# Hybrid decoder layer on one core: the order of the gating values, the layer norm by halves, chunk and attention steps by two token tiles, and staging of the last operands

## The chip, the cores and the metric

The kernel runs on one core of one Trainium2 chip. The metric is device time in microseconds of one launch; lower is better. The kernel before was timed three times: 2019.73, 2021.77 and 2022.76 us, so its median is 2021.77 us. One further execution was profiled.

## The reference, cut to what matters

One layer over 2048 tokens of 1024 features, all fp32. Two mixers share one input projection, one output projection and a residual; a SwiGLU block and a final norm follow.

```python
n = rms_norm(h, norm1_w)
q, k, v, g_lr, g_out, su, sv = split(n @ w_in)      # 256,256,512,16,512,512,512 columns
log_a = log_sigmoid(g_lr @ w_gate_up + b) / 16
# gated linear attention, 4 heads, chunks of 64 tokens
b = cumsum(log_a, in chunk); q_dec = q*exp(b); k_inv = k*exp(-b); k_end = k*exp(b_last-b)
o = causal(q_dec k_inv^T) v + q_dec S_prev          # S = exp(b_last)*S + k_end^T v, chunk by chunk
o_gla = rms_norm_per_head(o) * silu(g_out)
# spatial gating, 4 groups of 128 channels, chunks of 128 tokens
o_sg = gelu(su) * (tril(w_s) @ layer_norm_per_group(gelu(sv)) + b_s)
h = h + concat(o_gla, o_sg) @ w_out
h = h + (silu(n2 @ w_gate) * (n2 @ w_up)) @ w_down  # n2 = rms_norm(h); d_ff = 2816
return rms_norm(h, final_norm_w)
```

## The kernel before, in words

**Products.** Every fp32 operand is split into a high part (a cast on ACT, L103) and a low part (a subtraction on DVE, L104); a product is three matmuls, lines L124, L125 and L126 in turn. A matmul of 512 columns follows the one before after 0.227 us. The low part of a weight tile (`wlo`) is wanted by L125 or L124 of its first product, so TensorE waits for both ACT and DVE of each tile. Weight tiles come by DMA into `raw` (three slots), are split into a pool of four pairs, and are prepared in the order in which a list, `block_tiles`, names them.

**Stages.** The tokens are four blocks of 512, each four token tiles of 128. Blocks 0 and 1 go through `mix` and the output projection, then through gate, up and down together; blocks 2 and 3 likewise. Gate, up, down and (in blocks 1 to 3) the value and output-gate columns use a seven-product scheme (Winograd's form of Strassen's) on halves of the operands; the product numbers are `m`, taken for the values and the gate in the order 1, 2, 7, 6, 4, 5, 3. One product there is 24 matmuls with two weight tiles of 12.

**`mix`, in the order in which TensorE takes it in blocks 1 to 3.** First half of the gating values `sv` with the low-rank gate; the decay; the K pair of column tiles; the Q pair; the second half of `sv` (`second_half`, 96 matmuls of 256 columns); the seven products of values `v` and output gate `gw`; the `su` column pairs (`gate_pair`), between whose tiles the attention steps stand; the output projection. In block 0 values, second half and gate are plain products.

**Side work on DVE.** Behind the Q pair DVE scales the scans (L501 to L508), applies exponentials to Q and K (L516, L517) and writes `left` (L539). `sv_norm` (L611, L612, then the inverse root, which is L130 on DVE and L131 on POOL, then L616) normalises `sv`, one token tile a step. Products m=2, 4 and 5 are drained by DVE adds (L647, L653, L657); m=5 and m=3 accumulate in the same PSUM buffers, so m=3 waits for L657.

**Chunk and attention steps.** One `chunks` step per token tile: 16 hardware matmuls k_end^T v (L568), eight state updates on DVE (L577), 16 score matmuls (L584), two predicated copies into `left` (L588). The steps are a generator started by the drain of m=4 and advanced as tiles are used (`tick`); what is left is run by `finish` ahead of `su`. `attend` likewise: 16 matmuls (L690), ACT squares, the root on POOL, four scalings (L698), and two steps later four transposes (L677) into `mixT`, which the output projection reads (`mixTl` is its low part). L717 multiplies the normalised `sv` with the spatial weights.

**Order and last product.** The generators and a Tile scheduler fix the order on each engine; each engine then takes its instructions strictly in that order, and SP issues the DMAs. In the last `down` the a operand and the b operand (`load`, L916 and L921) both come through the three `raw` slots; hi and lo parts lie in a pool of 16 large tiles (`bigt`). The last product but one fetches up to five units ahead, since its operands and those of the last stay loaded.

Of the kernel before, what the change touches and what calls it, by code (L numbers as in the profile page):

```python
# [8 lines left out]
F32 = mybir.dt.float32  # L9
# [6 lines left out]
P = 128  # L16
D = 1024
T = 2048
NB = 512
# [14 lines left out]
def hybrid_block(ctx, tc, x, norm1_w, w_in, w_gate_up, b_gate_up, gla_norm_w, sg_ln_w, sg_ln_b,  # L34
# [15 lines left out]
    def ps():  # L50
        return psp.tile([P, 512], F32, name="ps", tag="ps")
# [384 lines left out]
    def block_tiles(blk, first):  # L436

        def vg(m, kk):
            at = {1: (0, C_V), 2: (4, C_V), 3: (4, C_GOUT)}.get(m)
            if at:  # L440
                return tok_load(w_in, [(at[1], 512)], at[0] + 2 * kk, 2)
            return load_w([vd[{5: 0, 7: 1, 4: 2, 6: 3}[m], 2 * kk:2 * kk + 2].rearrange("k p c -> p k c")], 2, 512)

        tiles = [] if first else tok_tiles(w_in, first_cols, 3)
        tiles += col_tiles(w_in, 256) + col_tiles(w_in, 0)
        second = tok_tiles(w_in, [(C_SV + 256, 256)], 4)
        if blk == 0:
            tiles += tok_tiles(w_in, [(C_V, 512)]) + second + tok_tiles(w_in, [(C_GOUT, 512)])
        else:
            tiles += second + [lambda m=m, kk=kk: vg(m, kk) for m in VG_ORDER for kk in range(2)]  # L450
        for i in range(2):
            tiles += col_tiles(w_in, C_SU + i * 2 * P)
        return tiles + tok_tiles(w_out, [(0, 512)], order=OUT_ORDER) + tok_tiles(w_out, [(512, 512)])

    def mix(blk, nT, first_w):
# [71 lines left out]
        def mine(hh):  # L527
            return slice(hh * DK, (hh + 1) * DK)
# [30 lines left out]


        def chunks():
            for t in range(TT):
                pu = [ps(), ps()]
                for c in range(2):
                    rows = slice(c * CH, (c + 1) * CH)
                    for h in range(HEADS):
                        p, hh = h // 2, h % 2
                        nc.tensor.matmul(pu[c][hh * DK:(hh + 1) * DK, p * DV:(p + 1) * DV],  # L568
                                         lhsT=kend[rows, t, p, hh * DK:(hh + 1) * DK],
                                         rhs=v[rows, t, h * DV:(h + 1) * DV], start=True, stop=True)  # L570
                for c in range(2):
                    n = 2 * t + c
                    for p in range(2):
                        for hh in range(2):
                            rows = mine(hh)
                            new = right(n + 1)[rows, hh, p] if n + 1 < NB // CH else state[rows, p]
                            nc.vector.scalar_tensor_tensor(new, right(n)[rows, hh, p], dec[rows, p, n:n + 1],  # L577
                                                           pu[c][rows, p * DV:(p + 1) * DV], ALU.mult, ALU.add)
                pq = [ps(), ps()]
                for p in range(2):  # L580
                    for c in range(2):
                        ts = slice((2 * t + c) * CH, (2 * t + c + 1) * CH)
                        for hh in range(2):
                            nc.tensor.matmul(pq[hh][other(hh), (2 * p + c) * CH:(2 * p + c + 1) * CH],  # L584
                                             lhsT=kinv[mine(hh), p, ts], rhs=left[mine(hh), hh, p, ts], start=True, stop=True)
                for hh in range(2):
                    rows = other(hh)
                    nc.vector.copy_predicated(left[rows, hh, :, t * P:(t + 1) * P].rearrange("q p (c i) -> q p c i", i=CH),  # L588
                                              keep_i[rows].unsqueeze(1).unsqueeze(1).to_broadcast([CH, 2, 2, CH]),
                                              pq[hh][rows, :4 * CH].rearrange("q (p c i) -> q p c i", c=2, i=CH))  # L590
                yield

        def chunks_start():
            values_put()
# [7 lines left out]
            tok_group(w_in, [(C_SV + 256, 256)], nT, ks=4,  # L602
                      done=lambda t, acc: nc.scalar.activation(sv[:, t, 256:512], acc[:, :256], AF.Gelu))

        def sv_norm():
            for t in range(TT):
                st = sm.tile([P, 4, 6], F32, name="bst")
                mv = sm.tile([P, 4, 2], F32, name="mv")
                rs = sm.tile([P, 4], F32, name="rs")
                for g in range(4):  # L610
                    nc.vector.bn_stats(st[:, g, :], sv[:, t, g * P:(g + 1) * P])  # L611
                    nc.vector.bn_aggr(mv[:, g, :], st[:, g, :])  # L612
                rsq(rs, mv[:, :, 1], 1, 4)
                for g in range(4):
                    sl = sv[:, t, g * P:(g + 1) * P]
                    nc.vector.tensor_scalar(sl, sl, mv[:, g, 0:1], rs[:, g:g + 1], ALU.subtract, ALU.mult)  # L616
                yield


        def gate_scale(t):  # L620
# [7 lines left out]
        if halves is None:  # L628
            tok_group(w_in, [(C_V, 512)], nT, done=lambda t, acc: nc.scalar.copy(v[:, t, :], acc))
            g_chunks = chunks_start()  # L630
            second_half()
            g_svn = start(sv_norm())
            gw = bigt(F32, "gw")
            tok_group(w_in, [(C_GOUT, 512)], nT, done=gate_done)
        else:
            second_half()
            g_svn = start(sv_norm())
            finish(g_half)
            gw = bigt(F32, "gw")
            started = []  # L640
# [21 lines left out]

            pair_product(halves, VG_ORDER, {1: 0, 6: 0, 5: 0, 3: 0, 2: 1, 7: 2, 4: 2}, drain)
            g_chunks = started[0]
        finish(g_chunks)
        finish(g_svn)


        mixT = Act(KD, "mixT")

        def attend():
            oms = []
            for t in range(TT + 2):
                if t >= 2:
                    pt = ps()
                    for h in range(HEADS):
                        nc.tensor.transpose(pt[:, h * P:(h + 1) * P], oms[t - 2][:, h * DV:(h + 1) * DV], ident)  # L677
                    mixT.put(0, t - 2, pt)
                if t >= TT:
                    yield  # L680
                    continue
                ss = sm.tile([P, HEADS], F32, name="ss")
                om, sq = tpt("om"), tpt("sq")
                oms.append(om)
                pos = [ps(), ps()]
                for p in range(2):
                    for hh in range(2):
                        for c in range(2):
                            n = 2 * t + c
                            nc.tensor.matmul(pos[hh][c * CH:(c + 1) * CH, p * DV:(p + 1) * DV],  # L690
                                             lhsT=left[:, hh, p, n * CH:(n + 1) * CH], rhs=right(n)[:, hh, p], start=True, stop=True)
                for h in range(HEADS):
                    p, hh = h // 2, h % 2
                    nc.scalar.activation(sq[:, :DV], pos[hh][:, p * DV:(p + 1) * DV], AF.Square, accum_out=ss[:, h:h + 1])
                rsq(ss, ss, DV, HEADS)
                for h in range(HEADS):
                    p, hh = h // 2, h % 2
                    nc.vector.scalar_tensor_tensor(om[:, h * DV:(h + 1) * DV], pos[hh][:, p * DV:(p + 1) * DV], ss[:, h:h + 1],  # L698
                                                   gw[:, t, h * DV:(h + 1) * DV], ALU.mult, ALU.mult)
                yield  # L700

        g_att = start(attend())

# [19 lines left out]
                split(h, l, mx)  # L723

        for i in range(2):
            gate_pair(i, col_pair(nT))
        return mixT, g_att, hx

    def residual(hx, dh, acc, t):
# [170 lines left out]
    def down(s):  # L900
# [9 lines left out]
            a = bigt(F32R, name).rearrange("p (x a) b -> p x a b", x=2)  # L910
            return a[:, 0, :k], a[:, 1, :k]

        def load(spare=False):
            m, j, k = grans.pop(0)
            raw = view(rawp, F32, "raw", k, NB)
            nc.sync.dma_start(raw, ad[s][m - 1, j:j + k].rearrange("j p t -> p j t"))  # L916
            a = unit_parts("aop", k)
            split(*a, raw)
            if spare:
# [22 lines left out]
        def run(nxt):  # L942
# [52 lines left out]
            for m in order:  # L995
# [156 lines left out]
```

## Time and profile before

| | |
|---|---|
| median of three runs | 2021.77 us |
| profiled execution, own time | 2024.96 us |
| its span | 2023.0 us |
| TensorE (PE) busy | 1977.1 us, 98% |
| VectorE (DVE) busy | 1503.8 us, 74% |
| ScalarE (ACT) busy | 890.4 us, 44% |
| GpSimd (POOL) busy | 92.2 us, 5% |
| mean granted TensorE clock | 0.995 |
| DMA engines, mean busy share | 50% |

The profiled execution is 3.2 us above the median and 2.0 us longer than its span. A row of a timeline gives the start, the busy time, the engine, the line, and in brackets the idle time just before it with what ended it. PEclk is the share of full clock granted in a stretch.

### The profile page before, as it was taken

What the parts mean: (1) busy time and instruction counts of PE and PEld (TensorE: products, weight loads), DVE (VectorE), ACT (ScalarE), POOL (GpSimd) and SP (SyncE); (2) the same over time, 40 slices, a digit from 0 to 9 for tenths busy, and PEclk for the clock granted to TensorE, in tenths of its full rate; (3) what the DMA queues carried; (4) which work ended last, traced back from release to release, by engine and by line L of the source; (5) the groups of instructions that cost most, each with busy time, mean ns of one, the idle gap of its engine ahead of it and who ended that gap; (6) DMA issues with size and microseconds to landing.
All of it is one profiled execution on the core that took longest, in us unless ns stands there. A gap on an engine that the chain in (4) does not pass through costs nothing. (4 is left out here: it accounts for less than half of the span.)

```text
span 2023.0 us, 26612 instructions
## 1 busy us (share of the span) xinstructions
PE 1977.1 (98%) x9837; PEld 1646.7 (81%) x9837; DVE 1503.8 (74%) x2529; ACT 890.4 (44%) x1454; POOL 92.2 (5%) x102
## 2 busy tenths in 40 slices
PE   7999999999999999999999999999999999999997
PEld 6878977888888888888788788788888888888886
DVE  5676988798887777655798768859977876866466
ACT  4534745453333333433565536446433333334334
POOL 1011100000000000000110102000000000000000
PEclk9999999999999999999999999999999999999999
DMA  7553585526653324865655534723332332367555
GB/s 233 167 202 101 198 249 195 182 89 203 209 162 99 125 89 142 292 196 185 238 177 160 174 116 160 215 85 119 122 107 86 126 101 85 124 209 253 195 165 178
DMA packets 216719, 329.28 MB, mean 163 GB/s; under 512 B 16599, under 2 KB 117645, under 8 KB 215566
## 3 DMA queue, kind: packets, MB, share of 16 engines
q1 hardware_dynamic: 216590, 327.59, 50.0%
q8 instruction: 77, 1.26, 0.3%
q14 instruction: 52, 0.43, 0.1%
HBM read 246.27 MB, written 77.07 MB: 160 GB/s over the span
## 5 line engine op out<-in xcount | busy, mean ns | idle before, releaser
L103 ACT CAST whi<-raw 128x1024 fp32r<-128x1024 f32 (+2 forms) x209 | 211.3, 1011 | 357.0 <-PE ps L125 143.1
L104 DVE TENSOR_TENSOR wlo<-raw,whi 128x1024 fp32r<-128x1024 f32 (+2 forms) x209 | 243.7, 1171 | 130.7 <-ACT whi L103 124.9
L124 PE MATMUL ps<-whi,aop 128*128 128x512 f32 x552 | 215.1, 390 | 1.2 <-DVE aop L104 1.2
L125 PE MATMUL ps<-wlo,aop 128*128 128x512 f32 x552 | 214.8, 389 | 0.6 <-DVE wlo L104 0.6
L126 PE MATMUL ps<-whi,aop 128*128 128x512 f32 x552 | 214.8, 389 | 0.0
L103 ACT CAST op<-sw 128x512 fp32r<-128x512 f32 x176 | 107.4, 622 | 200.0 <-DVE sw L787 180.0
L104 DVE TENSOR_TENSOR aop<-raw,aop 128x1024 fp32r<-128x1024 f32 x84 | 95.2, 1134 | 99.5 <-ACT aop L103 99.0
L104 DVE TENSOR_TENSOR op<-sw,op 128x512 fp32r<-128x512 f32 x176 | 120.0, 685 | 38.0 <-ACT op L103 37.6
L103 ACT CAST aop<-raw 128x1024 fp32r<-128x1024 f32 x84 | 82.0, 979 | 138.1 <-DMA raw<-ad 137.0
L124 PE MATMUL ps<-whi,nTl 128*128 128x512 f32 (+2 forms) x392 | 129.0, 329 | 3.4 <-DVE nTl L104 3.4
L125 PE MATMUL ps<-wlo,nTh 128*128 128x512 f32 (+2 forms) x392 | 127.4, 325 | 0.0
L126 PE MATMUL ps<-whi,nTh 128*128 128x512 f32 (+2 forms) x392 | 127.4, 325 | 0.0
L124 PEld LDWEIGHTS ps<-whi,aop 128*128 128x128 f32 x552 | 103.6, 188 | 23.1 <-ACT junk L136 1.6
L125 PEld LDWEIGHTS ps<-wlo,aop 128*128 128x128 f32 x552 | 103.6, 188 | 22.4 <-DVE wlo L104 0.9
L126 PEld LDWEIGHTS ps<-whi,aop 128*128 128x128 f32 x552 | 103.6, 188 | 21.3
L131 POOL TENSOR_TENSOR st<-st,half 128x1 f32<-128x1 f32 x48 | 45.5, 956 | 1481.0 <-DVE st L130 1450.9
L812 ACT COPY p<-ps 128x512 f32<-128x512 f32 x88 | 51.5, 588 | 137.4 <-PE ps L126 134.3
L124 PE MATMUL ps<-nTh,wlo 128*128 128x512 f32 x256 | 103.1, 403 | 6.3 <-DVE right L577 4.6
L104 DVE TENSOR_TENSOR op<-raw,op 128x512 fp32r<-128x512 f32 x132 | 88.5, 685 | 26.4 <-ACT op L103 25.9
L124 PE MATMUL ps<-whi,mixTl 128*128 128x512 f32 x256 | 102.0, 398 | 3.2 <-DVE mixTl L104 3.2
L126 PE MATMUL ps<-nTh,whi 128*128 128x512 f32 x256 | 100.7, 393 | 0.0
L125 PE MATMUL ps<-nTl,whi 128*128 128x512 f32 x256 | 100.6, 393 | 0.0
(257 smaller groups left out, 4963.4 us busy)
## 6 DMA issues: line engine op xcount, KB each, us to landing
raw<-ad SPq DMA_DIRECT2D x70, 512.0 KB, 3.9
raw<-in_w_in_dram SPq DMA_DIRECT2D x66, 512.0 KB, 4.1
raw<-in_w_ffn_gate_dram SPq DMA_DIRECT2D x44, 512.0 KB, 3.8
raw<-in_w_ffn_up_dram SPq DMA_DIRECT2D x44, 512.0 KB, 3.8
raw<-td SPq DMA_DIRECT2D x40, 512.0 KB, 4.5
ad<-cg SPq DMA_DIRECT2D x66, 256.0 KB, 2.0
ad<-cs SPq DMA_DIRECT2D x22, 768.0 KB, 3.6
hx<-in_x_dram SPq DMA_DIRECT2D x32, 512.0 KB, 6.9
```

Of the source, the lines that this page charges most:

```text
L103: nc.scalar.copy(hi, src)
L104: nc.vector.tensor_tensor(lo, src, f32(hi), ALU.subtract)
L124: nc.tensor.matmul(o, lhsT=ll, rhs=rh, start=first, stop=False, skip_group_check=shared)
L125: nc.tensor.matmul(o, lhsT=lh, rhs=rl, start=False, stop=False, skip_group_check=shared)
L126: nc.tensor.matmul(o, lhsT=lh, rhs=rh, start=False, stop=last, skip_group_check=shared)
L131: nc.gpsimd.tensor_tensor(dst, dst, half[:, :k], ALU.pow)
L812: nc.scalar.copy(t[m], o)
```

## The change

In blocks 1 to 3 the second half of `sv` goes behind the seven value and gate products. `sv_norm` is run twice, over two groups each time, with its own root per token tile: the first half may run as soon as the first columns are there, the second behind the second half; it is finished ahead of the `gate_pair` that reads it. `chunks` and `attend` issue the matmuls of two token tiles together, with a PSUM buffer shared by two tiles. In the last `down`, a load from the fifth on stages a and b in one large tile (`abraw`) in place of two `raw` slots.

```diff
-            tiles += second + [lambda m=m, kk=kk: vg(m, kk) for m in VG_ORDER for kk in range(2)]
+            tiles += [lambda m=m, kk=kk: vg(m, kk) for m in VG_ORDER for kk in range(2)] + second
...
         def chunks():
-            for t in range(TT):
-                pu = [ps(), ps()]
...
+            for t0 in range(0, TT, 2):
+                ts2 = (t0, t0 + 1)
+                pu, pq = [ps(), ps()], [ps(), ps()]
+                for i, t in enumerate(ts2):
...   # 16 matmuls k_end^T v each
+                for i, t in enumerate(ts2):
...   # 16 score matmuls each
+                for i, t in enumerate(ts2):
...   # 8 state updates, 2 predicated copies
+                    yield
...
-        def sv_norm():
+        def sv_norm(g0):
             for t in range(TT):
-                st = sm.tile([P, 4, 6], F32, name="bst")
+                st = sm.tile([P, 2, 6], F32, name="bst")
...
-                rsq(rs, mv[:, :, 1], 1, 4)
+                rsq(rs, mv[:, :, 1], 1, 2)
...
+        g_svn = [start(sv_norm(0))]
...
         else:
-            second_half()
-            g_svn = start(sv_norm())
             finish(g_half)
...
             pair_product(halves, VG_ORDER, {1: 0, 6: 0, 5: 0, 3: 0, 2: 1, 7: 2, 4: 2}, drain)
             g_chunks = started[0]
+            second_half()
+            g_svn.append(start(sv_norm(2)))
         finish(g_chunks)
-        finish(g_svn)
...
         def attend():
...
+            for t0 in range(0, TT, 2):
+                pos = [ps(), ps()]
...   # 32 matmuls for two token tiles
+                if t0:
+                    turn(t0 - 2)     # four transposes each
+                    turn(t0 - 1)
+                for i in range(2):
...   # squares, root, four scalings
                     yield
+            turn(TT - 2)
+            turn(TT - 1)
+            yield
...
-            gate_pair(i, col_pair(nT))
+            acc = col_pair(nT)
+            finish(g_svn[i])
+            gate_pair(i, acc)
...
-        def load(spare=False):
+        def load(spare=False, unit=False):
...
+            if unit:
+                u = bigt(F32, "abraw")
+                ra, rb = u[:, 0:k], u[:, 2:2 + k]
...
-                        load(len(loaded) >= 3)
+                        load(len(loaded) >= 3, len(loaded) >= 4)
...
-                            load(len(loaded) >= 4)
+                            load(True, True)
```

DVE in block 1, around the `left` writes behind the Q pair, in the kernel before; `wlo_2310`, `wlo_2368` and `wlo_2433` are the low parts of the first three value tiles, and the second half's two tiles were split earlier.

```order
L508 COPY dec_2075<-eu_2073 128x8
L104 TENSOR_TENSOR wlo_2310<-raw_2307,whi_2309 128x1024
L516 TENSOR_TENSOR eu_2073<-ps_2077,eu_2073 128x512
L517 TENSOR_TENSOR eu2_2074<-ps_2077,eu2_2074 128x512
L539 SCALAR_TENSOR_TENSOR left_2221<-ps_2226,eu_2073 64x512 x2
L539 SCALAR_TENSOR_TENSOR left_2221<-ps_2227,eu_2073 64x512 x2
L104 TENSOR_TENSOR wlo_2368<-raw_2365,whi_2367 128x1024
L407 TENSOR_TENSOR nw_3831<-nw_3831 128x256
L409 TENSOR_TENSOR nw_3831<-nw_3831 128x256
L410 TENSOR_TENSOR nw_3831<-nw_3831 128x256
L104 TENSOR_TENSOR wlo_2433<-raw_2430,whi_2432 128x1024
```

There the second value tile is split right behind `left`, and the third behind three small sums of the down weights. The same place after the change, where `wlo_2339` is the fourth value tile, `wlo_2372` and `wlo_2390` are the tiles of m=7, and L651 is the add that drains m=2:

```order
L502 SCALAR_TENSOR_TENSOR bc_2213<-carry_156,la_2212 128x512
L504 TENSOR_TENSOR la_2212<-bc_2213 128x512
L539 SCALAR_TENSOR_TENSOR left_2229<-ps_2234,eu_2081 64x512
L508 COPY dec_2083<-eu_2081 128x8
L516 TENSOR_TENSOR eu_2081<-ps_2085,eu_2081 128x512
L517 TENSOR_TENSOR eu2_2082<-ps_2085,eu2_2082 128x512
L539 SCALAR_TENSOR_TENSOR left_2229<-ps_2234,eu_2081 64x512
L539 SCALAR_TENSOR_TENSOR left_2229<-ps_2235,eu_2081 64x512 x2
L104 TENSOR_TENSOR wlo_2339<-raw_2336,whi_2338 128x1024
L104 TENSOR_TENSOR wlo_2372<-raw_2369,whi_2371 128x1024
L104 TENSOR_TENSOR wlo_2390<-raw_2387,whi_2389 128x1024
L651 TENSOR_TENSOR v_2314<-ps_2367,v_2314 128x512
```

Three value tiles are now split ahead of these rows, and the fourth stands behind the last `left` write, on which it does not depend; the four steps of the first half's norm stand further ahead, before the scan.

TensorE at the end of the seven products of block 1 in the kernel before, from the last matmul of m=3 to the first of `su`:

```order
L126 MATMUL ps<-whi,hop 128x512
L568 MATMUL ps<-v,eu_2074 64x128 x8
L584 MATMUL ps<-left,eu 64x64 x8
L568 MATMUL ps<-v,eu_2074 64x128 x8
L584 MATMUL ps<-left,eu 64x64 x8
L124 MATMUL ps<-nTh_1502,wlo 128x512
L125 MATMUL ps<-nTl_1504,whi 128x512
```

And after the change (L570 and L579 are the two chunk lines):

```order
L126 MATMUL ps<-whi,hop 128x512
L570 MATMUL ps<-v,eu_2082 64x128 x16
L579 MATMUL ps<-left,eu 64x64 x16
L124 MATMUL ps<-whi,nTl_1512 128x256
L125 MATMUL ps<-wlo,nTh_1510 128x256
L126 MATMUL ps<-whi,nTh_1510 128x256
```

The second half, with 256 columns, now stands between the last chunk step and `su`; the other two steps stand together ahead of m=5, where before one stood ahead of m=5 and one ahead of m=3.

DVE in block 1 ahead of the drain of m=5 (L657) in the kernel before, from the updates of the first chunk step on:

```order
L577 SCALAR_TENSOR_TENSOR right1_2223<-right0_2222,dec_2075,ps_2710 64x128 x4
L577 SCALAR_TENSOR_TENSOR right0_2222<-right1_2223,dec_2075,ps_2711 64x128 x4
L588 COPY_PREDICATED left_2221<-keep_161,ps_2728 64x2x128
L588 COPY_PREDICATED left_2221<-keep_161,ps_2729 64x2x128
L104 TENSOR_TENSOR wlo_2815<-raw_2812,whi_2814 128x1024
L657 TENSOR_TENSOR gw_2427<-ps_2428,gw_2427 128x512
```

The same after the change (L588 state update, L592 predicated copy, L661 the drain of m=5):

```order
L588 SCALAR_TENSOR_TENSOR right1_2231<-right0_2230,dec_2083,ps_2578 64x128 x4
L588 SCALAR_TENSOR_TENSOR right0_2230<-right1_2231,dec_2083,ps_2579 64x128 x4
L592 COPY_PREDICATED left_2229<-keep_161,ps_2580 64x2x128
L592 COPY_PREDICATED left_2229<-keep_161,ps_2581 64x2x128
L588 SCALAR_TENSOR_TENSOR right1_2231<-right0_2230,dec_2083,ps_2578 64x128 x4
L588 SCALAR_TENSOR_TENSOR right0_2230<-right1_2231,dec_2083,ps_2579 64x128 x2
L661 TENSOR_TENSOR gw_2315<-ps_2316,gw_2315 128x512
```

The drain of m=5 stands behind 14 state updates and two copies of the same double step; before, behind eight updates, two copies and a weight tile's split, with a chunk step on TensorE to wait beside.

## Rows read from the trace of the kernel before

**Rows 1.** The page, busy time of TensorE

```profile
PE   1977.1 (98%) x9837; PEld 1646.7 (81%) x9837; DVE 1503.8 (74%) x2529; ACT 890.4 (44%) x1454; POOL 92.2 (5%) x102
```

**Rows 2.** What TensorE waited for: total, times, longest (us)

```profile
PE ps L124 <- DVE right L577: 4.6, 6, 1.5
...
PE ps L124 <- DVE mixTl L104: 3.2, 4, 1.2
...
PE ps L124 <- DVE gw L657: 2.5, 3, 1.5
...
PE ps L568 <- DVE right L577: 0.6, 1, 0.6
```

**Rows 3.** Timeline of TensorE, block 1, ahead of m=3

```profile
289.13 1.06 PE L568 MATMUL ps<-v,eu 64*64 64x128 f32 x16
292.06 0.33 PE L584 MATMUL ps<-left,eu 64*64 64x64 f32 x2 [1.87 <-DVE right L577]
293.57 1.12 PE L584 MATMUL ps<-left,eu 64*64 64x64 f32 x14 [1.19 <-DVE right L577]
296.20 0.77 PE L124 MATMUL ps<-whi,hop 128*128 128x512 f32 x1 [1.52 <-DVE gw L657]
...
297.62 0.63 PE L124 MATMUL ps<-whi,hop 128*128 128x512 f32 x1
298.05 0.63 PE L125 MATMUL ps<-wlo,hop 128*128 128x512 f32 x1
```

**Rows 4.** Timeline of TensorE, block 2, single and double chunk step

```profile
1109.28 0.68 PE L568 MATMUL ps<-v,eu 64*64 64x128 f32 x16
...
1111.20 0.47 PE L124 MATMUL ps<-whi,hop 128*128 128x512 f32 x1 [0.79 <-DVE gw L657]
...
1116.83 0.68 PE L568 MATMUL ps<-v,eu 64*64 64x128 f32 x16
...
1120.38 0.50 PE L124 MATMUL ps<-nTh,wlo 128*128 128x512 f32 x1 [1.48 <-DVE right L577]
```

**Rows 5.** Stretches: window, us, PE busy, PEclk, DMA share, GB/s

```profile
1107.00:1127.00 20.00, 17.41 (x150) 0.91 0.83 234
...
1149.00:1156.00 7.00, 7.00 (x54) 1.00 0.24 76
```

**Rows 6.** Timeline of TensorE, first matmul behind the Q pair, blocks 1 and 2

```profile
242.62 0.28 PE L124 MATMUL ps<-whi,nTl 128*128 128x256 f32 x1
...
1062.30 0.28 PE L124 MATMUL ps<-whi,nTl 128*128 128x256 f32 x1
```

**Rows 7.** Timeline of DVE, the last `left` writes, blocks 1 and 2

```profile
248.10 2.80 DVE L539 SCALAR_TENSOR_TENSOR left<-ps,eu 64x512 f32<-64x512 f32 x4
...
1068.93 2.12 DVE L539 SCALAR_TENSOR_TENSOR left<-ps,eu 64x512 f32<-64x512 f32 x3
```

**Rows 8.** Groups by line: busy, mean ns, idle before and releaser

```profile
L616 DVE TENSOR_SCALAR sv<-sv,mv,rs 128x128 f32<-128x128 f32 x64 | 19.0, 342 | 13.7 <-POOL rs L131 13.7
```

**Rows 9.** Timeline of DVE, block 1, one chunk step

```profile
290.53 2.99 DVE L577 SCALAR_TENSOR_TENSOR right<-right,dec,ps 64x128 f32<-64x128 f32 x8
293.44 0.91 DVE L588 COPY_PREDICATED left<-keep,ps 64x256 f32<-64x256 int32 x2
294.25 1.21 DVE L104 TENSOR_TENSOR wlo<-raw,whi 128x1024 fp32r<-128x1024 f32 x1
295.38 1.27 DVE L657 TENSOR_TENSOR gw<-ps,gw 128x512 f32<-128x512 f32 x2
```

**Rows 10.** Timeline of TensorE, the last down products

```profile
1989.64 0.50 PE L125 MATMUL ps<-bop,aop 128*128 128x512 f32 x1 [0.96 <-DVE bop L104]
...
1994.00 0.50 PE L124 MATMUL ps<-bop,aop 128*128 128x512 f32 x1 [1.57 <-ACT bop L103]
1995.26 0.50 PE L125 MATMUL ps<-bop,aop 128*128 128x512 f32 x1 [0.76 <-DVE bop L104]
```

**Rows 11.** Chain that ended last, same place: start, us, what

```profile
1987.15 5.73 DMA raw<-td
```

More of the change, by code (lines that the diff above doesn't have):

```diff
@@ L561, in chunks @@
         def chunks():
-            for t in range(TT):
-                pu = [ps(), ps()]
[L564 to L572, printed above, removed]
-                    for p in range(2):
[L574 to L580, printed above, removed]
-                    for c in range(2):
[L582 to L591, printed above, removed]
@@ L635, in mix @@
         else:
-            second_half()
-            g_svn = start(sv_norm())
             finish(g_half)
@@ L664, in mix @@
             g_chunks = started[0]
+            second_half()
+            g_svn.append(start(sv_norm(2)))
         finish(g_chunks)
-        finish(g_svn)
         mixT = Act(KD, "mixT")
         def attend():
[L672 to L675, printed above, removed]
-                    for h in range(HEADS):
-                        nc.tensor.transpose(pt[:, h * P:(h + 1) * P], oms[t - 2][:, h * DV:(h + 1) * DV], ident)
-                    mixT.put(0, t - 2, pt)
-                if t >= TT:
-                    yield
[L681 to L700, printed above, removed]
@@ new lines, in attend, with turn @@
+            oms = [None] * TT
+            def turn(t):
+                pt = ps()
+                for h in range(HEADS):
+                    nc.tensor.transpose(pt[:, h * P:(h + 1) * P], oms[t][:, h * DV:(h + 1) * DV], ident)
+                mixT.put(0, t, pt)
+            for t0 in range(0, TT, 2):
+                pos = [ps(), ps()]
+                for i in range(2):
+                    for p in range(2):
+                        for hh in range(2):
+                            for c in range(2):
+                                n = 2 * (t0 + i) + c
+                                nc.tensor.matmul(pos[hh][c * CH:(c + 1) * CH, (2 * i + p) * DV:(2 * i + p + 1) * DV],
+                                                 lhsT=left[:, hh, p, n * CH:(n + 1) * CH], rhs=right(n)[:, hh, p], start=True, stop=True)
+                if t0:
+                    turn(t0 - 2)
+                    turn(t0 - 1)
+                for i in range(2):
+                    t = t0 + i
+                    ss = sm.tile([P, HEADS], F32, name="ss")
+                    om, sq = tpt("om"), tpt("sq")
+                    oms[t] = om
+                    for h in range(HEADS):
+                        p, hh = h // 2, h % 2
+                        nc.scalar.activation(sq[:, :DV], pos[hh][:, (2 * i + p) * DV:(2 * i + p + 1) * DV], AF.Square, accum_out=ss[:, h:h + 1])
+                    rsq(ss, ss, DV, HEADS)
+                    for h in range(HEADS):
+                        p, hh = h // 2, h % 2
+                        nc.vector.scalar_tensor_tensor(om[:, h * DV:(h + 1) * DV], pos[hh][:, (2 * i + p) * DV:(2 * i + p + 1) * DV], ss[:, h:h + 1],
+                                                       gw[:, t, h * DV:(h + 1) * DV], ALU.mult, ALU.mult)
+                    yield
@@ L911, in unit_parts @@
             return a[:, 0, :k], a[:, 1, :k]
-        def load(spare=False):
+        def load(spare=False, unit=False):
             m, j, k = grans.pop(0)
-            raw = view(rawp, F32, "raw", k, NB)
-            nc.sync.dma_start(raw, ad[s][m - 1, j:j + k].rearrange("j p t -> p j t"))
-            a = unit_parts("aop", k)
-            split(*a, raw)
-            if spare:
+            if unit:
+                u = bigt(F32, "abraw")
+                ra, rb = u[:, 0:k], u[:, 2:2 + k]
+            else:
+                ra = view(rawp, F32, "raw", k, NB)
+            nc.sync.dma_start(ra, ad[s][m - 1, j:j + k].rearrange("j p t -> p j t"))
+            if unit:
+                nc.sync.dma_start(rb, right[m][:, j:j + k])
+            a = unit_parts("aop", k)
+            split(*a, ra)
+            if unit:
+                b = unit_parts("bop", k)
+                split(*b, rb)
+            elif spare:
                 raw = view(rawp, F32, "raw", k, NB)
```

37 lines of the change are left out of this document (31 added, 6 removed).

## Prediction

> **What bounds the kernel now.** I read the page's busy times first: TensorE is busy for 1977.1 of 2023.0 us [rows 1], so a change of order can return at most the 46 us in which it is idle, plus what a halved clock costs. The table of TensorE's waits says next whom it waits for [rows 2]. The part that this change touches is small: waits on the chunk steps' state updates, on the drain `gw` and on the low part of `mixT`. The timelines say where these lie. In block 1 the matmuls of one chunk step wait 1.87 and 1.19 us for updates that still hold PSUM buffers, and m=3 then waits 1.52 us for the drain of m=5 [rows 3]. The 1.87 + 1.19 = 3.06 us there, the 4.6 us of L124 on the updates and the 2.5 us on `gw` [rows 2, 3] make 10.2 us over blocks 1 to 3. Blocks 2 and 3 have a double chunk step directly ahead of `su`, which `su` then pays for; in block 2 it is 1.48 us [rows 4].
>
> The clock falls there too. Behind the waits of block 1 matmuls stand 0.43 us apart [rows 3] where 0.227 is normal. These are rows at 1.2 GHz; the mean over block 2's stretch is 0.91 against 1.00 in a quiet one [rows 5]. Last I read the end: TensorE waits 0.96, 1.57 and 0.76 us for operands [rows 10], and the chain goes back from there to a DMA of 5.73 us, which could start only when a `raw` slot was given back [rows 11].
>
> **Chunk steps, blocks 1 to 3.** The 10.2 us go, because the second half, 96 matmuls of 256 columns or about 11 us, now stands between the last double step and `su`. DVE's work for a double step is twice 2.99 + 0.91 us [rows 9], 7.8 us, which fits beside it. With the waits the two half-clock spells go: about eight matmuls each at 0.43 - 0.227, 1.6 us, and in block 1 the step's own matmuls, which run at half speed as well. From 289.13 to 296.20 less 4.58 of waits leaves 2.49 us [rows 3], against 1109.28 to 1111.20 less 0.79, 1.13 us, in block 2 [rows 4]: 1.4 us more. Together 4.6. Joining two steps saves their joints. A single one takes 1.13 + 0.1 of lead; a double one, from 1116.83 to 1120.38 less 1.48, takes 2.07 + 0.1 [rows 4]. That is 0.28 a pair, and one pair a block is new: 0.8.
>
> **A wait that stays.** m=3 uses the buffers of m=5 and has no chunk step ahead of it any more. From the end of m=4 TensorE needs 2.2 us for the double step and 24 x 0.227 = 5.45 for m=5. DVE gets the first sums after about 1.1 us and then does eight updates 2.99, two copies 0.91, six updates 2.24 and the first add 0.64 [rows 9], and perhaps a split of 1.21: 7.9 to 9.1 us. So m=3 waits 0.2 to 1.5 us; I take 1.3, as in block 1 before, for each of three blocks: 3.9.
>
> **A wait that is new.** Value tiles are used up in 12 x 0.227 = 2.73 us each, directly behind Q. The fourth is wanted 3 x 2.73 + 0.23 = 8.4 us behind Q's end: at 251.0 in block 1 and 1070.7 in block 2 [rows 6]. Its split stands behind the last `left` write on DVE, which ended at 250.9 and 1071.05 [rows 7]. Adding 1.21 us of split [rows 9] gives waits of 1.1 and 1.6 us, mean 1.35, or 4.0 for three blocks (block 3 taken as their mean). This is if DVE reaches `left` as early as before. The first half's norm now lies ahead of the scan, and each of its four round trips to POOL can hold DVE: 13.7 us over 16 trips [rows 8], 0.86 each, up to 3.4 a block. DVE in that stretch waits for ACT anyway, so I take one trip, 0.8, a block: 6.5 us in all, with bounds 4.0 and 14.3.
>
> **New clock spells.** Each idle piece beside small matmuls may bring a spell of 1.6 us. Two of six places had one; the six new waits are of the same size. I take 1.6 spells, 2.6 us, between 0 and 9.6.
>
> Blocks 1 to 3 come to -10.2 - 4.6 - 0.8 + 3.9 + 6.5 + 2.6 = -2.6 us.
>
> **Block 0 and attention.** In block 0 a wait of 0.6 us goes [rows 2], and two pairs are joined, 0.6, with about 0.4 for a step that ran slow beside it: -1.6. Its values are plain products; the order there is otherwise kept. The last attention matmuls of every block move one weight tile (5.45 us) ahead, at the price of two roots in a row behind them, so the 3.2 us of `mixTl` waits [rows 2] mostly go: -2.8 (between -1.0 and -3.2). Joined attention steps save nothing else that I can see.
>
> **The end.** The units take a and b in one tile, so that a load waits for no `raw` slot. The three waits are 3.3 us [rows 10], and a half-clock spell of 1.6 follows. The last operand of m=4 can lie only where an output tile has been written out, since the pool of 16 is full; I take 0.9 back and keep -4.0 (between +1 and -4.9: SP's queue now holds loads behind two output DMAs, as it did one before). The 512 KB loads are the same in number.
>
> **The sum.** -2.6 - 1.6 - 2.8 - 4.0 = -11.0 on the profiled 2024.96: 2014 us. The profiled execution is 3.2 above the median, so I forecast 2011 us. Everything else (gate, up, the first down, output projection) keeps its order; the norm by halves adds 16 trips to POOL, one more per token tile, and those of the second half lie beside `su`.
>
> **A rule against the change.** In block 2's attention steps four transposes and 32 other small matmuls run without a break, and the stretch around them is granted 1.00 [rows 5]; the new order puts eight transposes and 32 attention matmuls in one piece. The Trainium skill, page "TensorE: Matmul & The Clock Gate", section "Part 4: PE-mode transpose", says that transposes do not count as busy for the clock as other matmuls do. By that rule, longer runs of them would drop the clock; the trace with half as many in a row does not show it.
>
> **Rivals.**
> *DVE's queue takes it all back (slower).* One mechanism: the first half's norm and the value splits lie in one queue with the scan, and TensorE waits for the fourth value tile. For it: nothing but the queue's order ties the split to `left`, and [rows 8] show trips that hold DVE for 0.86 us. Against it: DVE idles in that stretch. Its price is 3.4 a block beyond the 4.0, and the value and gate tiles behind it wait as well, 1.21 a tile: some 4.5 + 1.6 for a spell more a block than I took, 18 in all. That gives 2029; it decides from 3.7 us a block more (then nothing is gained).
> *The waits go fully.* The splits are in time because the scan starts earlier than before, and no spell is left: 6.5 + 2.6 less, 2002. For it: the first value tiles are split before the exponentials. Against it: the fourth waits behind `left` in any case.
> *The clock falls in the longer runs of small matmuls.* Two attention pieces a block, eight at 1.6 us: 12.8 on top, 2024, no change that can be seen.
> *The end does not move.* If the output tiles hold the last operands, 4 us stay: 2015, inside the forecast's own range.
>
> **Chances.** The forecast with its own range, 2005 to 2017, 0.58; waits fully gone 0.14; DVE's queue 0.13; clock 0.06; other losses of a similar size (a wait of DVE on a DMA of down weights ahead of the drains) 0.09. I call 0.2%, 4 us, what a measurement can tell from no change. Faster by more: the forecast nearly whole (0.55), the full gain 0.14 and a little of the mixed case make 0.71. Within: 0.16, from the clock, the mixed case and weak forms of DVE's queue. Slower: 0.13. The range is 2000 to 2021; it leaves out the strong form of DVE's queue and a gain above 21 us.
>
> **What would show it.** In the profile after, TensorE's waits on updates (L577 before) should fall from 7.7 us to under 1, `mixTl` to under 1, and the last down's three waits to under 1.5. New should be a wait of L125 on `wlo` in each of blocks 1 to 3, 1 to 3 us, some 8 us behind Q's end, with `left` the last thing on DVE ahead of the split, and a wait of m=3 on the drain of m=5, near 1.3. `su` should have no wait ahead of it. It would be wrong if the `wlo` waits sum to over 12, if half-clock spells stand behind the attention pieces, or if `sv`'s second half, normalised late, holds the spatial matmuls (L717 before).

## The result and the profile after

Four runs of the changed kernel take 2008.15 to 2012.75 us, median 2010.31; four of the kernel before in the same session 2019.73 to 2022.76, median 2020.93. The ratio is 0.9947, with a 95% interval of 0.993 to 0.9964: 10.7 us faster (7.3 to 14.1). The forecast was 2011, in a range of 2000 to 2021.

The page of the changed kernel, the row that answers to [rows 1]:

```profile
span 2006.4 us, 26606 instructions
...
PE 1964.3 (98%) x9837; PEld 1642.1 (82%) x9837; DVE 1505.4 (75%) x2545; ACT 885.5 (44%) x1451; POOL 95.9 (5%) x118
```

The profiled spans differ by 16.6 us, the medians by 10.6. The profiled execution of before was longer than all four of its timed runs, that of after was the fastest of its four. So terms are read from the traces by stage, and the total from the medians.

What TensorE waited for after the change (total, times, longest), to be held against [rows 2]:

```profile
PE ps L124 <- DVE gw L661: 6.8, 3, 3.6
PE ps L124 <- DVE mixTl L104: 4.6, 3, 2.0
...
PE ps L125 <- DVE wlo L104: 3.2, 4, 1.5
```

The waits on the chunk steps' updates (7.7 us before) are gone, as are the three at the end. The waits on the drain of m=5 grew from 2.5 to 6.8, those on `mixTl` from 3.2 to 4.6, and a wait on the low part of value tiles is new.

The same 8544 large matmuls run in both kernels, so a stage can be cut at the start of the same matmul in both timelines. Length of the stages in us:

| stage | before | after | change |
|---|---|---|---|
| block 0, from the second half of `sv` to `su` | 40.18 | 37.81 | -2.4 |
| blocks 1, 2, 3, from Q's end to `su` | 63.72, 58.08, 57.03 | 61.29, 58.77, 58.00 | -0.8 |
| blocks 0 to 3, `su` with attention | 31.10, 31.83, 33.44, 31.85 | 30.35, 30.38, 30.38, 30.38 | -6.7 |
| blocks 0 to 3, first 96 matmuls of output projection | 25.09, 23.52, 25.06, 23.48 | 25.83, 24.54, 25.00, 23.21 | +1.4 |
| end, from the matmul at 1985 us of before to the last one | 30.56 | 24.50 | -6.1 |

That is -14.5. The other 2.0 of the 16.6 lie in stages whose order did not change: mostly at the start (45.83 against 44.63 from the first large matmul to the values of block 0, where the clock of before is halved from 33.5 to 36.9 us) and in gate, up and down of the first blocks.

How far one execution can be trusted shows from a second one. The kernel called "the first half's norm later" below turned out to hold the same instructions in the same order as the changed kernel on TensorE, DVE, ACT and POOL. Its profiled execution took 2014.9 us. The rows of the table would there read -2.4, -0.1, -6.7, +5.1 and -6.1, together -10.2. Its waits are

```profile
PE ps L124 <- DVE gw L663: 5.6, 3, 2.5
PE ps L124 <- DVE mixTl L104: 5.1, 3, 2.0
```

and the clock is halved in four places of these stages (from 164.0, 283.4, 344.9 and 1102.6 us on), where the first has one (from 279.6 on). The kernel without staging tiles, whose TensorE order is the same too, gives 6.3 and 4.9 for the two waits and two such places.

The longer wait in block 1, TensorE at the start of m=3 (compare [rows 3]):

```profile
275.93 0.39 PE L126 MATMUL ps<-whi,hop 128*128 128x512 f32 x1
279.89 0.77 PE L124 MATMUL ps<-whi,hop 128*128 128x512 f32 x1 [3.57 <-DVE gw L661]
280.46 0.63 PE L125 MATMUL ps<-wlo,hop 128*128 128x512 f32 x1
...
282.59 0.58 PE L124 MATMUL ps<-whi,hop 128*128 128x512 f32 x1
283.01 0.40 PE L125 MATMUL ps<-wlo,hop 128*128 128x512 f32 x1
```

And DVE beside it:

```profile
270.65 0.42 DVE L407 TENSOR_TENSOR nw<-nw 128x256 f32<-128x256 f32 x1 [1.19 <-DMA nw<-in_w_ffn_down_dram]
271.00 0.68 DVE L657 TENSOR_TENSOR v<-ps,v 128x512 f32<-128x512 f32 x1
271.60 0.41 DVE L549 COPY eu<-ps 128x256 f32<-128x256 f32 x1
271.93 1.22 DVE L104 TENSOR_TENSOR wlo<-raw,whi 128x1024 fp32r<-128x1024 f32 x1
273.06 3.00 DVE L588 SCALAR_TENSOR_TENSOR right<-right,dec,ps 64x128 f32<-64x128 f32 x8
275.97 0.91 DVE L592 COPY_PREDICATED left<-keep,ps 64x256 f32<-64x256 int32 x2
276.79 2.24 DVE L588 SCALAR_TENSOR_TENSOR right<-right,dec,ps 64x128 f32<-64x128 f32 x6
279.06 0.69 DVE L661 TENSOR_TENSOR gw<-ps,gw 128x512 f32<-128x512 f32 x1
```

The eight updates, two copies and six updates take the 2.99 + 0.91 + 2.24 us that the forecast had, but they start at 273.06, behind a sum of down weights that waited for its DMA, the add of m=4, a copy and a split. TensorE loses 3.57 us and runs about seven matmuls at half clock. In blocks 2 and 3 the wait is 1.64 and 1.55. The second execution bears this out: there L407 did not wait for its DMA, 1.19 us in the first, and block 1's wait is 2.45, 1.12 less.

### The profile page after: what moved, and what is told of

It reads as the page before. It is cut to its first block, busy times and chain, and to the rows that moved or that the text cites. A ratio compares the mean times of both kernels' runs of the same rounds, so it can differ in the third digit from the quotient of the medians.

```text
span 2006.4 us, 26606 instructions
## 1 busy us (share of the span) xinstructions
PE 1964.3 (98%) x9837; PEld 1642.1 (82%) x9837; DVE 1505.4 (75%) x2545; ACT 885.5 (44%) x1451; POOL 95.9 (5%) x118
## 5 line engine op out<-in xcount | busy, mean ns | idle before, releaser
L104 DVE TENSOR_TENSOR aop<-raw,aop 128x1024 fp32r<-128x1024 f32 x76 | 86.6, 1139 | 92.8 <-ACT aop L103 92.4
L104 DVE TENSOR_TENSOR op<-sw,op 128x512 fp32r<-128x512 f32 x176 | 120.6, 688 | 36.9 <-ACT op L103 36.5
L103 ACT CAST aop<-raw 128x1024 fp32r<-128x1024 f32 x76 | 74.6, 985 | 125.3 <-DMA raw<-ad 124.3
L126 PE MATMUL ps<-whi,mixTh 128*128 128x512 f32 x256 | 99.8, 390 | 0.0
```

Source lines behind the costliest of these rows:

```text
L103: nc.scalar.copy(hi, src)
L104: nc.vector.tensor_tensor(lo, src, f32(hi), ALU.subtract)
L126: nc.tensor.matmul(o, lhsT=lh, rhs=rh, start=False, stop=last, skip_group_check=shared)
```

## Experiments

Every kernel was timed against the kernel before in its own session, whose median there lay between 2022.8 and 2023.7. So ratios are compared.

**The staging tiles alone, and all but them.** The first kernel has the last hunks of the change, the second all others.

```diff
-                        load(len(loaded) >= 3)
+                        load(len(loaded) >= 3, len(loaded) >= 4)
...
-                            load(len(loaded) >= 4)
+                            load(True, True)
```

> The kernel before with the large staging tiles of the last down alone. My theory: the last product's three operand waits (3.3 us) and the half-clock spell behind them (1.6) go and nothing else changes: 4 to 6 us less than before, 2015 to 2017, with the waits of blocks 1 to 3 as before. Rival: the waits at the end of the profiled execution of before were an accident of that execution, or come back as a wait for output tiles: within 1.5 us of before, 2019.5 to 2021.

> The changed kernel with the loads of the last down as before. My theory: the parts are independent, so this costs what the staging tiles gave: 4 to 6 us more than the changed kernel, 2014.5 to 2016.5, with three operand waits of about 3 us in all near the end. Rival (the staging tiles give nothing): 2010 to 2011.5. Rival (they gave nearly all of it): 2018 or more.

Measured: alone 2014.81 us, ratio 0.9962 (0.9949 to 0.9975); without them 2014.62, ratio 0.9953 (0.994 to 0.9967). In the trace of the first the end takes 24.48 us against 30.56 of before, and the stages of blocks 1 to 3 are as before within 0.7 us, but for a half-clock spell that block 2 is spared. In the second it takes 29.25 and the waits are back. What TensorE waited for near the end there:

```profile
PE ps L125 <- DVE bop L104: 1.8, 3, 0.8
PE ps L124 <- ACT bop L103: 1.3, 2, 0.7
```

By the stages the staging tiles give 4.8 to 6.1 us at the end, and the parts act in different places. The timed runs are less clear. The tiles alone give 7.7 us on before; without them the kernel is still 9.5 faster, only 1.2 behind the changed one, which is where the rival that they give nothing would have it (2011.4 us against the first session's 2020.93). Each interval reaches some 2.7 us to either side, so by these times alone neither the tiles' worth inside the changed kernel nor the independence of the parts is shown; the trace of the end decides for the tiles.

**Attention steps of one token tile.** The changed kernel with `attend` as before.

```diff
-            for t0 in range(0, TT, 2):
-                pos = [ps(), ps()]
...
+            for t in range(TT + 2):
...
+                pos = [ps(), ps()]
```

> The changed kernel with attention steps of one token tile as before. My theory (two roots in a row make the low part of mixT late): the waits on mixTl fall from 4.6 us to about 3, but the joints of the small matmuls come back (9.9 against 9.1 us a block, 3 us in all): 2011 to 2012.5. Rival (joined steps save nothing on TensorE and only delay mixT): 2008 to 2009.5. Rival (mixTl waits come from other work on DVE): they stay at 4 us or more and the time is 2013 to 2014.

Measured: 2012.88 us, ratio 0.9946 (0.9932 to 0.9959), so the change in time cannot be told from none. The trace tells more: the `su` stages take 31.11 and three times 31.13 us, 0.75 longer each than with joined steps, and the waits on `mixTl` fall to

```profile
PE ps L124 <- DVE mixTl L104: 2.8, 3, 1.2
```

but a new one of 2.3 us on ACT's `su` stands in block 1, where the changed kernel waits 1.48 on `mixTl`, and the clock is halved behind it; with it block 1's output projection is the longer one here, 52.28 us to 49.03. By block, single steps take 0.8 off the wait of block 0, change nothing in block 2 and add 0.4 in block 3. Joining the steps saves 3.0 us in the `su` stages; that it returns 1.8 in the output projection is not shown.

**The first half's norm later.** In blocks 1 to 3 the source starts it with the drain of m=2.

```diff
-        g_svn = [start(sv_norm(0))]
+        g_svn = [start(sv_norm(0))] if halves is None else []
...
                     nc.vector.tensor_tensor(v[:, lo, :], acc, v[:, lo, :], ALU.add)
+                    if th:
+                        g_svn.append(start(sv_norm(0)))
```

> The changed kernel with the first half's norm of blocks 1 to 3 started by the drain of m=2, behind the scan and left. My theory of the new wait on value tiles (the norm's trips to POOL hold DVE ahead of left): the waits on wlo behind Q, 2.7 us in three blocks, fall under 0.8, and nothing else changes: 12 to 13.5 us less than before. Rival (the fourth tile waits for the scan and left alone): they stay at 2 us or more, 10 to 11 less than before. Rival (norm work now delays the drains or the spatial matmuls): less than 10 less.

Measured: 2011.61 us, ratio 0.9947 (0.9936 to 0.9959), the same as the changed kernel. This is a failed experiment: the edit of the source left the order of the instructions as it was. In blocks 1 and 3 all eight scalings of the first half's norm still start 4.0 us or more ahead of Q's end. So the waits behind Q, 0.34, 1.48 and 0.85 us against 0.35, 1.46 and 0.85, tell nothing on the theory; the run is a repeat of the changed kernel.

The trace of the changed kernel says something on it. The last L501, the step of the scan that the last `left` writes wait behind, stands behind the norm in blocks 1 and 3, and there and in block 2 DVE was idle for ACT ahead of it:

```profile
240.07 0.69 DVE L501 TENSOR_TENSOR la<-la,ab 128x512 f32<-128x512 f32 x1 [0.44 <-ACT ab L500]
...
1056.53 0.69 DVE L501 TENSOR_TENSOR la<-la,ab 128x512 f32<-128x512 f32 x1 [1.59 <-ACT ab L500]
...
1233.38 0.69 DVE L501 TENSOR_TENSOR la<-la,ab 128x512 f32<-128x512 f32 x1 [1.23 <-ACT ab L500]
```

And the longest wait, 1.46 us, is in block 2, where six of the eight scalings come only behind `left`. So the norm can hardly be what sets these waits; whether it adds to them in blocks 1 and 3 no run shows.

**The chunk steps started by m=5.**

```diff
                 elif m == 4:
...
-                    if th:
-                        started.append(chunks_start())
                 elif m == 5:
...
+                    if th:
+                        started.append(chunks_start())
```

> The changed kernel with the chunk steps started by the drain of m=5 in place of m=4, so that a double step stands between m=5 and m=3 and its updates stand on DVE behind the drain of m=5. My theory: the waits of m=3 for that drain (6.8 us in three blocks) and the half-clock spell behind the longest one (1.3) go, and the second double step is covered by the second half: 2001 to 2004. Rival (DVE is simply short of time there, so the wait moves to su or to the second double step): 2007 to 2011, with waits of su or of the chunk matmuls on updates of 4 us or more. Rival (slower: steps too late for attention): above 2011.

Measured: 2014.41 us, ratio 0.9954 (0.9942 to 0.9967). The waits on the drain are gone, and from Q's end to `su` blocks 1 to 3 take 55.65, 56.75 and 56.15 us, 9.5 us less than in the changed kernel. All of it comes back:

```profile
PE ps L124 <- DVE mixTl L104: 10.7, 4, 3.7
...
PE ps L692 <- DVE om L708: 1.9, 1, 1.9
```

and half-clock spells begin at 164.0, 344.9, 1037.8 and 1160.7 us; the first is in block 0, which the edit leaves alone, and the third stands behind a wait on a weight tile at the start of block 2's K pair, so these two cannot be put down to it. The last state updates now end 0.4 to 3.1 us behind the start of `su`, in place of 6.2 to 7.1 ahead, all of the second half's norm comes behind them, and the first attention scalings of blocks 1 to 3 start 3.4 to 4.7 us later. The last rival held, in time and in mechanism: steps too late for attention.

**Chunk steps of one token tile.** The changed kernel with `chunks` as before.

```diff
-            for t0 in range(0, TT, 2):
-                ts2 = (t0, t0 + 1)
-                pu, pq = [ps(), ps()], [ps(), ps()]
...
+            for t in range(TT):
+                pu = [ps(), ps()]
```

> The changed kernel with chunk steps of one token tile as before, so that in blocks 1 to 3 a step stands between m=5 and m=3 again and the last one inside the second half. My theory (m=3 waits because nothing covers the drain of m=5): the waits on that drain fall from 6.8 us to 2.5 or less and the half-clock spell behind goes, while the joints come back (2.2 us in block 0, about 0.6 a block in 1 to 3): 11 to 13.5 us less than before, that is 0.5 to 2.5 better than the changed kernel. Rival (DVE's backlog, not the cover, sets the drain): the waits stay near 7 and the time is 6 to 8 us less than before.

Measured: 2007.5 us, ratio 0.9922 (0.9909 to 0.9935), 15.8 less than before, more than the theory had. By the ratios it is 5.1 us better than the change itself, though the two intervals just overlap. With a step between m=5 and m=3 the waits on the drain are

```profile
PE ps L124 <- DVE gw L657: 0.5, 1, 0.5
```

and the stages from Q's end to `su` take 58.39, 57.48 and 56.99 us, against 61.29, 58.77 and 58.00; block 0 pays 1.7 for the joints. What m=3 lacked was cover. By the stages, joining the chunk steps costs 5.2 us in blocks 1 to 3 (4.5 to 5.8 against the other two traces of the changed order) and saves 1.7 in block 0.

**The second half between m=5 and m=3.** The list of weight tiles is put in the same order, which the cut leaves out.

```diff
                 elif m == 5:
...
+                    if th:
+                        second_half()
+                        g_svn.append(start(sv_norm(2)))
...
             g_chunks = started[0]
-            second_half()
-            g_svn.append(start(sv_norm(2)))
```

> The changed kernel with the second half of the gating values between m=5 and m=3 in blocks 1 to 3, by the drain of m=5, chunk steps as in the changed kernel. My theory: 11 us of the second half cover the drain of m=5 and the updates without making the chunk steps later, so the waits of m=3 (6.8 us) and the spell (1.3) go and none takes their place: 16 to 19 us less than before. Rival (as with the chunk steps started by m=5: DVE's backlog reaches the output projection): the waits on mixTl grow by 4 us or more, 9 to 13 less than before.

Measured: 2005.12 us, ratio 0.9914 (0.9901 to 0.9927). In its trace the waits on the drain are gone, and from Q's end to `su` blocks 1 to 3 take 57.72, 56.89 and 56.19 us, 7.3 less than in the changed kernel. The first double step stands where it did. The updates of the second end 1.7 to 2.1 us behind the start of `su`, as late as in the run above that started the steps by m=5, but three of the four steps of the second half's norm now stand ahead of them, and attention's first scalings start only 0.7 to 2.0 us later than in the changed kernel. What TensorE waits for now, on `mixTl` and once, in block 1, in the middle of the second half:

```profile
PE ps L124 <- DVE mixTl L104: 5.2, 3, 2.1
...
PE ps L124 <- DVE right L589: 1.8, 1, 1.8
```

My theory held for the time, 17.4 us on before by the timed runs, and for the waits of m=3; that no wait takes their place is wrong by 1.8 us.

**Two edits on that kernel.** `left` is written a step behind m=1; the operands of the gate stage start two ticks later; and both.

```diff
-        for p in range(2):
-            for hh in range(2):
+        def left_put():
+            yield
+            for p in range(2):
+                for hh in range(2):
...
+        g_left = start(left_put())
...
             yield
             yield
+            yield
+            yield
             operand(1, b1[0])
```

> The kernel with the second half between m=5 and m=3, and with the writes of left given by a step behind m=1 in place of directly behind Q, so that the split of the fourth value tile stands on DVE ahead of most of them. My theory now (that split waits in DVE's queue behind left and the scan, whatever the norm does): the waits on wlo behind Q (2.7 us) fall under 0.7, 2 us less than without, that is 19 to 20.5 us less than before. Rival (the split waits for its cast on ACT or its DMA): they stay above 2 us, 17 to 18 us less than before.

> The kernel with the second half between m=5 and m=3, and with the operands of the gate stage cast and split two weight tiles later in the output projection of blocks 1 and 3. My theory (the low part of mixT is late since casts on ACT and splits on DVE for the gate stage stand ahead of its own): the wait on mixTl in block 1 (2.2 us) falls under 1, with 0 to 2 us less time, while those of blocks 0 and 2 (1.95 and 1.14), which have other work there, stay: 17.5 to 19.5 less than before. Rival (mixTl is late because attention ends late): block 1's wait stays at 1.5 us or more, 16.5 to 18 less. Rival (the operands then come late for the gate stage): a new wait there of 2 us or more.

> Both of these edits together on the kernel with the second half between m=5 and m=3. If the two waits are independent, the gains add: 20 to 22.5 us less than before. If they share DVE's backlog, one moves into the other: 18 to 19.5 less.

Measured: 2007.23 us, ratio 0.992 (0.9907 to 0.9933); 2006.81, 0.9921 (0.9908 to 0.9933); both 2009.68, 0.9935 (0.9922 to 0.9947). With `left` late the waits on `wlo` behind Q are gone in all three blocks, which shows that the split waited in DVE's queue behind `left`. But others take their place, as TensorE's waits in that kernel show:

```profile
PE ps L124 <- DVE mixTl L104: 6.6, 3, 3.5
PE ps L587 <- DVE v L666: 3.9, 2, 2.2
```

By the timed runs nothing is gained over 2005.12 us, ratio 0.9914. The second edit is a failed experiment: its trace has the same instructions in the same order as the kernel that it was made on, and the wait of block 1 is 2.36 us. It tells nothing on its theory, and the kernel with both edits has the order of the one with late `left`. So the last two ratios repeat kernels already timed, and their distance from these, 0.0007 and 0.0015 or up to 3 us, is what timing one order twice gives here.

**One root for two token tiles.** On the kernel with the second half between m=5 and m=3.

```diff
-                for i in range(2):
-                    t = t0 + i
-                    ss = sm.tile([P, HEADS], F32, name="ss")
+                ss = sm.tile([P, 2 * HEADS], F32, name="ss")
+                for i in range(2):
...   # the squares of both tiles
-                    rsq(ss, ss, DV, HEADS)
+                rsq(ss, ss, DV, 2 * HEADS)
+                for i in range(2):
...   # the scalings of both tiles
```

> The kernel with the second half between m=5 and m=3, and in attention one root for both token tiles of a step (eight squares, one trip to POOL, eight scalings). In the changed kernel ACT's squares of the second tile wait 3.2 to 3.6 us for DVE's scalings of the first. My theory now (two roots one behind the other make the chain to mixT late): mixTl waits fall from 5.2 us to under 3 and that in block 1 from 2.2 to under 0.5, 18.5 to 20.5 us less than before. Rival (the position of mixT's own casts and splits in the queues of ACT and DVE, behind the spatial half and next work, sets them): they stay above 4 us, 17 to 18 less than before.

The expectation rests on ACT in the changed kernel, block 1: four squares of the first tile, then a wait for DVE's scalings of it ahead of the squares of the second. Its timeline, and its waits:

```profile
325.54 0.30 ACT L704 ACTIVATE sq<-ps 128x128 f32<-128x128 f32 x1
325.70 0.22 ACT L704 ACTIVATION_READ_ACCUMULATOR sq<-ps 128x1 f32 x1
329.25 0.28 ACT L704 ACTIVATE sq<-ps 128x128 f32<-128x128 f32 x1 [3.33 <-DVE om L708]
```

```profile
ACT sq L704 <- DVE om L708: 22.9, 8, 4.8
```

Measured: 2001.14 us, ratio 0.9893 (0.9875 to 0.9911), the best kernel here; its interval lies below that of the change. (ACT's eight waits of this kind in the changed kernel are 2.2 to 4.8 us, not 3.2 to 3.6.) ACT's wait is gone from its list, and TensorE's is

```profile
PE ps L124 <- DVE mixTl L104: 1.9, 2, 1.2
```

with 0.76 us in block 0, 1.16 in block 1 and none in blocks 2 and 3. So the two roots one behind the other, with ACT's wait between them, made the larger part of `mixT`'s lateness. The edit does two things, one root in place of two and all squares ahead of all scalings; which of them counts was not separated. The wait in block 1 did not fall under 0.5 as expected, and what holds it is open. The wait on the updates inside the second half of block 1 stays, 2.0 us.

## Why the prediction was right

**Chunk steps (-10.2 of waits, -4.6 of clock).** Right. No wait on their updates is left, `su` starts without one in every block, and both half-clock spells of those places are gone. One reading in it was off: of the 1.4 us that it put down to the clock in block 1's own step, 0.4 belong to L568, whose 16 matmuls took 1.06 us [rows 3] at a granted clock of 1.00. With the three costs that follow, blocks 1 to 3 were to give -2.6; up to the end of `su`, without the 0.75 a block of joined attention (below), they gave -4.5, and -3.9 in the second execution.

**The wait that stays (3.9).** Right in its mechanism, too small: 6.8. Blocks 2 and 3 gave 1.64 and 1.55 for 1.3; block 1 gave 3.57, since DVE came to the updates late, in part by the wait for a DMA of down weights that the forecast names among its other losses. The one-tile chunk steps and the moved second half both remove it, but for 0.5 us in the first, by putting work on TensorE ahead of m=3.

**The wait that is new (6.5).** Right in its mechanism, 2.7 in size; the 1 to 3 us set as its sign for each block came in block 2 alone. With the norm's delay left out the forecast had 1.1 and 1.6 for blocks 1 and 2, and 0.35 and 1.46 came. The added 0.8 a block did not come: `left` ended 7.6 us behind Q's end in block 1 against 8.3 before, 8.7 in block 2 against 8.75 [rows 6, 7], and 8.1 in block 3 against 7.6, in blocks 1 and 3 with the norm's trips ahead of it. That the split waits behind `left` the run with late `left` shows; what the norm adds no run shows. The rival that DVE's queue takes it all back fell, since the waits are small.

**New clock spells (2.6).** One came in blocks 1 to 3 up to `su`, behind the longest wait; the second execution of this order has two there and two more in the output projection. The number is chance in one execution.

**The low part of `mixT` (-2.8).** Wrong in sign: the waits grew by 1.4. The step that failed is "at the price of two roots in a row behind them, so the 3.2 us of `mixTl` waits [rows 2] mostly go". The attention matmuls did move ahead, but the price was the larger part: ACT waited 2.9 us a time for the first tile's scalings. The run with one root shows it, with waits of 1.9 in place of 5.2. The sign set for it, `mixTl` under 1, missed.

**Attention (0).** Wrong: "Joined attention steps save nothing else" missed 0.75 us a block, 3.0 in all, shown by the steps of one tile. It makes up for a good part of the last error.

**Block 0 (-1.6).** -2.4 by the stage.

**The end (-4.0).** -6.1. The term was mis-sized: nothing had to be taken back for the last operand, since no wait stands at the end any more, and the waits cost more than their idle time. From 1992.04 to 1994.00 a wait of 1.57 us costs 1.96 less the normal 0.227, 1.73; the one of 0.96 costs 1.24 and its next matmul 0.11 more.

**The clock in longer runs of small matmuls.** Fell. The stretches with 32 attention matmuls and eight transposes in one piece:

```profile
319.00:326.00 7.00, 7.00 (x60) 1.00 0.26 88
1132.00:1139.00 7.00, 7.00 (x60) 1.00 0.36 124
1308.00:1315.00 7.00, 7.00 (x60) 1.00 0.40 120
```

The clock stays at 1.00. The rule on transposes in "TensorE: Matmul & The Clock Gate" of the Trainium skill, section "Part 4: PE-mode transpose", does not show in these stretches.

By the traces the stages of the change gave -14.5 in one execution and -10.2 in the other, against the -11.0 forecast; by the medians it is -10.6. Errors of both signs met: the output projection came out 4.2 us worse than forecast (7.9 in the second execution, with its clock spells), and blocks 1 to 3 (-1.9 or -1.3), block 0 (-0.8), attention (-3.0) and the end (-2.1) better. So the direction and most mechanisms were right, and that the time came within 1 us of 2011 is luck. Of the terms sized from waits that stood in the trace, those on chunk steps and the end held in direction and the one on `mixTl` did not.

## What to carry to other kernels

When work is moved to cover one wait, ask what it covered where it stood: here m=3 lost the chunk step that hid the drain of m=5, and putting the moved work exactly there gave 6.7 us more by the ratios. Joining steps pays in joints on the engine that bounds and costs in chains on the others; count both, and share what is on the chain (one root for two tiles), not only the matmuls. On an in-order engine that is short of time a wait that is removed by delaying its work turns up at the next consumer, as twice here. And read the order of the instructions in the trace before the time: a scheduler can undo an edit of the source, as it seems to have done with two edits here, in three runs, whose times measure only the spread.

## What the runs showed of the hardware

Two waits of TensorE near the end cost 0.16 and 0.39 us more than the idle time in their rows (1.73 for 1.57; 1.24 and 0.11 for 0.96): a 512-column matmul shows 0.39 us but follows the one before after 0.227, and the one behind a wait was followed after 0.34.

The clock did not answer the same wait the same way each time. In the output projection of block 0 TensorE waits 1.95 to 1.97 us for `mixTl` in nine of these profiles. In seven the granted clock is 0.5 (1.2 GHz) behind it, and the stage 1.6 us longer; in two, the changed kernel and the one with chunk steps of one token tile, it stays at 1.00 (2.4 GHz). In the other four the wait is 0.76 or 1.17, and the clock stays.

Runs of one kernel differ by 2 to 8 us, and stages of unchanged code by up to 3.9: the first, from the first large matmul to the values of block 0, took 43.6 to 46.7 us over these traces, and gate, up and down of blocks 0 and 1 took 634.9 to 638.8. So one profiled execution's total says less than its stages, and two executions of one order say more than one.
